# Moving all but three DMA issues of a transpose kernel from SyncE to ScalarE's own queue

## The chip, the cores and the metric

One core of one Trainium2 chip. The time is device microseconds of one execution; the median of several is given. The kernels were checked for the right result on the chip.

## The reference

```python
def setup_inputs():
    return {"x": np.random.randn(8192, 8192).astype(np.float32)}

def reference(x):
    return np.transpose(x)
```

256 MiB in, 256 MiB out, no arithmetic.

## The kernel before

The input is cut into two column halves of 4096 columns, and each half into 64 chunks of 128 rows: 128 chunks, each loaded by one DMA of 2 MiB into one of three input buffers. TensorE transposes a chunk in eight groups of four 128x128 tiles, each group into one of eight PSUM tiles. ScalarE copies the even groups out of PSUM and VectorE the odd ones, into output regions that gather eight chunks, so that the rows written to memory are 4 KB long. In each ordinary chunk one region is complete and is stored by one DMA of 2 MiB; there are nine regions for eight open ones. SyncE issues all loads and stores, in the order store of chunk t, load of chunk t+3.

The loop, cut to what the change touches (`# ...` marks cuts):

```python
def load(t):
    s, c = chunks[t]
    nc.sync.dma_start(
        out=ins[t % NIN], in_=x[c * P:(c + 1) * P, s * J:(s + 1) * J]
    ).then_inc(s_ld[t % NIN], 16)

for t in range(NIN):          # NIN = 3
    load(t)
# ...
for t, (s, c) in enumerate(chunks):
    nc.tensor.wait_ge(s_ld[t % NIN], 16 * (t // NIN + 1))
    closing = []
    for q in [(c + k) % NR for k in range(NR)]:
        if q not in window:
            # ... take a region r; if it was used before:
            (nc.scalar, nc.vector)[q % 2].wait_ge(s_st[r], 16 * stored[r])
        # ... wait for the PSUM tile, four transposes, last.then_inc(s_pe, 1); n += 1
        (nc.scalar, nc.vector)[e].wait_ge(s_pe, n)       # e = q % 2
        # ... copy to the region, then_inc(s_cp[e], 1)
        if t + 1 == t0 + sum(z - a for _, a, z in parts):
            closing.append((q, e, copied[e]))
    for q, e, count in closing:
        nc.sync.wait_ge(s_cp[e], count)
        # ... one DMA per part of the region, on nc.sync
    if t + NIN < len(chunks):
        nc.sync.wait_ge(s_pe, n)
        load(t + NIN)
```

At the seam between the two column halves a region belongs to both, and is stored by two DMAs with shorter rows.

## Time and profile before

| | before |
|---|---|
| time | 1265.68 us median of 3 (1265.38 to 1265.71) |
| profiled span | 1263.6 us |
| bytes moved by the kernel | 536.9 MB, plateau about 429 GB/s |
| busy: TensorE, VectorE, ScalarE | 59%, 28%, 24% |
| load, issue to landing (median) | 23.6 us |
| full-size store, issue to landing (median) | 22.6 us |

How to read it: "issue to landing" is the time from the instruction that starts a DMA to its last completion signal, "slice" a fortieth of the span, "plateau" the slices at a steady rate, and "the pipe" the DMA engines taken together. The compute engines are far from busy (59% at most), the DMA engines are busy in every slice (90% or more in 39 of 40, 80% or more in the last). The prediction below shows the lines.

### The profile page before, as it was taken

Reading aid. Unit: us, or ns where it says so; the run is one execution under the profiler, and the core shown is the slowest. Engines: PE = TensorE matmul, PEld = TensorE weight load, DVE = VectorE, ACT = ScalarE, POOL = GpSimd, SP = SyncE. Lnnn points to the kernel's source line nnn. Section 1 sums busy time; section 2 is a strip of 40 time slices with the busy share of each in tenths; the row PEclk is TensorE's granted clock in tenths of the full one; section 3 lists DMA queues with packets and bytes.
Section 4 is the critical chain, followed back from the end, with each engine's and each line's share of the span. In section 5 each row is a group of like instructions: output and inputs, shape, how many; then the busy total and the mean of one; then the engine's idle time right before and its main releaser. Section 6 shows DMA issues by size and latency. Waiting matters only on the chain.

```text
span 1263.6 us, 9807 instructions
## 1 busy us (share of the span) xinstructions
PE 748.9 (59%) x4096; PEld 724.9 (57%) x4096; DVE 353.9 (28%) x512; ACT 301.2 (24%) x513; POOL 0.7 (0%) x6
## 2 busy tenths in 40 slices
PE   6666555665566656565566655665556656565561
PEld 5566555665566656565566655665555655565551
DVE  3322222232222322222222322222222322223220
ACT  3222222222222222222222222222222222222220
POOL 0000000000000000000000000000000000000000
PEclk9876868677677776868677767777777686868776
DMA  9999999999999999999999999999999999999998
GB/s 385 427 427 430 428 427 430 429 430 429 428 428 428 430 429 429 428 430 429 427 427 412 430 429 428 429 429 429 429 429 429 429 429 427 431 429 429 430 427 351
DMA packets 39308, 537.51 MB, mean 425 GB/s; under 512 B 4320, under 2 KB 4832, under 8 KB 6240
## 3 DMA queue, kind: packets, MB, share of 16 engines
q1 hardware_dynamic: 39264, 536.89, 99.9%
q8 instruction: 32, 0.52, 0.2%
q14 instruction: 12, 0.10, 0.0%
HBM read 268.44 MB, written 268.44 MB: 425 GB/s over the span
## 4 chain that ended last, share of the span: by engine, by line
DMA 78%; PE 19%; issue 0%; ACT 0%; SPq 0%; ACTq 0%
DMA in<-in_x_dram 78%; PE ps L139 19%; ACT reg L150 0%; SPq L209 0%; SPq L69 0%; ACTq L148 0%
## 5 line engine op out<-in xcount | busy, mean ns | idle before, releaser
L139 PE MATMUL ps<-ident,in 128*128 128x128 f32 x4096 | 748.9, 365 | 486.8 <-DMA in<-in_x_dram 486.8
L139 PEld LDWEIGHTS ps<-ident,in 128*128 128x128 f32 x4096 | 724.9, 219 | 510.7 <-DMA in<-in_x_dram 502.4
L152 DVE COPY reg<-ps 128x512 f32<-128x512 f32 x512 | 353.9, 691 | 882.1 <-PE ps L139 882.1
L150 ACT COPY reg<-ps 128x512 f32<-128x512 f32 x512 | 299.9, 586 | 934.3 <-PE ps L139 932.6
L150 ACT ACT_TABLE_LOAD x1 | 1.3, 1283 | 0.9 <-SPq L69 0.9
L84 POOL TENSOR_SCALAR_AFFINE_SELECT ident<-ident 128x128 f32<-128x128 f32 x1 | 0.3, 292 | 0.2 <-POOL ident L82 0.2
L82 POOL MEMSET ident<- 128x128 f32 x1 | 0.2, 204 | 0.5 <-SPq L69 0.5
L198 POOL MEMSET const-bfloat16-1.0<- 128x1 bf16 x1 | 0.1, 101 | 0.0
L198 POOL MEMSET const-uint8-127<- 128x1 uint8 x1 | 0.1, 101 | 0.0
L198 POOL MEMSET const-float32-0.0<- 128x1 f32 x1 | 0.1, 98 | 0.2 <-issue 0.2
L198 POOL MEMSET const-float32-1.0<- 128x1 f32 x1 | 0.1, 98 | 0.0
## 6 DMA issues: line engine op xcount, KB each, us to landing
in<-in_x_dram SPq DMA_DIRECT2D x128, 2048.0 KB, 23.6
out_dram<-reg SPq DMA_DIRECT2D x114, 2048.0 KB, 22.6
out_dram<-reg SPq DMA_DIRECT2D x4, 1792.0 KB, 19.9
out_dram<-reg SPq DMA_DIRECT2D x4, 1536.0 KB, 19.6
out_dram<-reg SPq DMA_DIRECT2D x4, 1280.0 KB, 19.6
out_dram<-reg SPq DMA_DIRECT2D x4, 1024.0 KB, 19.4
out_dram<-reg SPq DMA_DIRECT2D x4, 768.0 KB, 17.9
out_dram<-reg SPq DMA_DIRECT2D x4, 512.0 KB, 16.2
```

Source lines behind the costliest of these rows:

```text
L82: nc.gpsimd.memset(ident, 0.0).then_inc(s_id, 1)
L84: nc.gpsimd.affine_select(out=ident, in_=ident, compare_op=mybir.AluOpType.not_equal, fill=1.0, base=0, pattern=[[-1, P]], channel_multipl ...
L139: last = nc.tensor.transpose(ps[:, b * P:(b + 1) * P], ins[t % NIN][:, q * B * P + b:(q + 1) * B * P - B + b + 1:B], ident,)
L150: cp = nc.scalar.copy(out=o, in_=i)
L152: cp = nc.vector.tensor_copy(out=o, in_=i)
L198: nc = _bacc.Bacc("TRN2", target_bir_lowering=False, num_devices=1)
```

## The change

The intent, in the words that came with it: loads and stores are all issued by ScalarE on its own queue, and SyncE issues only the first three loads and holds almost no program. ScalarE issues a finished region's store after its next copy, so that it never waits for the copy it has just started.

```diff
-            nc.sync.dma_start(
+            (nc.sync if t < NIN else nc.scalar).dma_start(
                 out=ins[t % NIN], in_=x[...]
...
+        def store(q, e, count):
+            t0, r, parts = window.pop(q)
+            nc.scalar.wait_ge(s_cp[e], count)
+            # ... the same DMAs as before, on nc.scalar ("qActDynamicHW")
+            free.append(r)
...
                 cp.then_inc(s_cp[e], 1)
+                if e == 0:
+                    for k in closing:
+                        store(*k)
+                    closing = []
                 if t + 1 == t0 + sum(z - a for _, a, z in parts):
                     closing.append((q, e, copied[e]))
-            for q, e, count in closing:
-                nc.sync.wait_ge(s_cp[e], count)
-                # ... the DMAs on nc.sync
+            for k in closing:
+                store(*k)
             if t + NIN < len(chunks):
-                nc.sync.wait_ge(s_pe, n)
+                nc.scalar.wait_ge(s_pe, n)
                 load(t + NIN)
```

More of the change, by code (lines that the diff above doesn't have):

```diff
@@ L111 @@
         window = {}
-        stores = 0
+        def store(q, e, count):
+            t0, r, parts = window.pop(q)
+            nc.scalar.wait_ge(s_cp[e], count)
+            base = 0
+            for s, a, z in parts:
+                rows = (z - a) * P
+                j0 = s * J + q * B * P
+                dst = out[j0:j0 + B * P, a * P:a * P + rows]
+                dst = dst.rearrange("(q b) i -> q b i", q=P)
+                src = regs[r][:, base:base + B * rows]
+                base += B * rows
+                if any(stored):
+                    st = wide_dma(nc, nc.scalar, "qActDynamicHW", dst, src)
+                else:
+                    st = nc.scalar.dma_start(
+                        out=dst, in_=src.rearrange("q (b i) -> q b i", b=B)
+                    )
+                st.then_inc(s_st[r], 16)
+                stored[r] += 1
+            free.append(r)
         for t, (s, c) in enumerate(chunks):
@@ L155 @@
                 bank[(n - 1) % NPS] = (s_cp[e], copied[e])
+                if e == 0:
+                    for k in closing:
+                        store(*k)
+                    closing = []
                 if t + 1 == t0 + sum(z - a for _, a, z in parts):
                     closing.append((q, e, copied[e]))
-            for q, e, count in closing:
-                t0, r, parts = window.pop(q)
-                nc.sync.wait_ge(s_cp[e], count)
-                base = 0
-                for s_, a, z in parts:
-                    rows = (z - a) * P
-                    j0 = s_ * J + q * B * P
-                    dst = out[j0:j0 + B * P, a * P:a * P + rows]
-                    dst = dst.rearrange("(q b) i -> q b i", q=P)
-                    src = regs[r][:, base:base + B * rows]
-                    base += B * rows
-                    if stores:
-                        st = wide_dma(nc, nc.sync, "qSPDynamicHW", dst, src)
-                    else:
-                        st = nc.sync.dma_start(
-                            out=dst, in_=src.rearrange("q (b i) -> q b i", b=B)
-                        )
-                    st.then_inc(s_st[r], 16)
-                    stores += 1
-                    stored[r] += 1
-                free.append(r)
+            for k in closing:
+                store(*k)
             if t + NIN < len(chunks):
-                nc.sync.wait_ge(s_pe, n)
+                nc.scalar.wait_ge(s_pe, n)
                 load(t + NIN)
```

## The prediction

> **What bounds the kernel now.** I read the page first (busy shares, slices, DMA queues, chain), then the waits of the compute engines and of SyncE's queue, then the chain in order of time, then the timeline around one ordinary chunk of rows, one chunk at the seam between the two column halves, and the tail.
>
> The page of the kernel before:
>
> ```profile
> span 1263.6 us, 9807 instructions
> PE 748.9 (59%) x4096; PEld 724.9 (57%) x4096; DVE 353.9 (28%) x512; ACT 301.2 (24%) x513; POOL 0.7 (0%) x6
> ...
> DMA  9999999999999999999999999999999999999998
> GB/s 385 427 427 430 428 427 430 429 430 429 428 428 428 430 429 429 428 430 429 427 427 412 430 429 428 429 429 429 429 429 429 429 429 427 431 429 429 430 427 351
> ...
> q1 hardware_dynamic: 39264, 536.89, 99.9%
> q8 instruction: 32, 0.52, 0.2%
> q14 instruction: 12, 0.10, 0.0%
> ```
>
> No compute engine is over 60% busy; the DMA row is full in every slice. The 536.89 MB of queue 1 at the plateau of 429 GB/s need 1251.5 us. The span is 12.1 us longer: the first slice (31.6 us at 385 instead of 429) loses 3.2 us, the last (351) 5.7 us, slice 22 (412) 1.3 us, and the slices at 427 and 428 the rest. The kernel is a full transfer pipe with a start, an end and one small dip.
>
> The chain of waits names loads (78%) and TensorE (19%), which could be misread as a latency problem: a load can be issued only when TensorE has finished the chunk that lay in its buffer, three chunks earlier. In order of time:
>
> ```profile
> 347.55 6.50 PE ps L139 x32
> 354.07 22.71 DMA in<-in_x_dram
> 376.83 5.60 PE ps L139 x32
> 382.45 23.61 DMA in<-in_x_dram
> 406.11 6.28 PE ps L139 x32
> 412.40 22.94 DMA in<-in_x_dram
> ```
>
> The columns are start, length, what. TensorE's part varies with the granted clock, from 5.60 to 6.50 us, and the load's part gives it back: 6.50 + 22.71 = 29.21, 5.60 + 23.61 = 29.21, 6.28 + 22.94 = 29.22. A load issued 0.9 us later lands at the same moment. The turn is 3 x 9.74 us, three chunks at the pipe's pace: one chunk moves 2.10 MB in and 2.10 MB out, 4.19 MB / 429 GB/s = 9.78 us. So 23 us from issue to landing is not latency but queue: 23.6 us x 429 GB/s = 10.1 MB, 2.4 chunks of work in front of every new transfer. This is a natural experiment on exactly what the change does, and I lean on it most.
>
> The waits, compute engines first, then SyncE's queue (us in total, times, longest):
>
> ```profile
> ACT reg L150 <- PE ps L139: 932.6, 510, 7.3
> PE ps L139 <- DMA in<-in_x_dram: 486.8, 127, 8.3
> ACT reg L150 <- DMA out_dram<-reg: 1.7, 2, 1.1
> ...
> SPq L99 <- PE ps L139: 467.1, 125, 8.8
> SPq L28 <- DVE reg L152: 318.8, 65, 9.2
> ```
>
> ScalarE idles 932.6 us for TensorE, so it has room; it waited only twice, 1.7 us in all, for a store to free an output region.
>
> [...]
>
> **The change, part by part.**
>
> 1. Issue time moves. SyncE loses 125 loads and 142 stores. An ordinary store issue takes 0.545 us (the median of the tile view of the output), a load issue 0.34 us: 142 x 0.545 + 125 x 0.34 = 120 us. ScalarE's 301 us become about 421 us, 33% of the span. Off the path: 0.
>
> 2. Stores leave later. Each chunk closes one region, with its first group. Before, SyncE issues as soon as that copy is done; now ScalarE issues after its next copy. An ordinary chunk before:
>
> ```profile
> 611.07 6.20 PE L139 MATMUL ps<-ident,in 128*128 128x128 f32 x32 [4.16 <-DMA in<-in_x_dram]
> 612.23 0.59 ACT L150 COPY reg<-ps 128x512 f32<-128x512 f32 x1 [4.65 <-PE ps L139]
> 612.85 1.22 SPq L28 DMA_DIRECT2D out_dram<-reg  x2
> 613.09 0.69 DVE L152 COPY reg<-ps 128x512 f32<-128x512 f32 x1 [5.93 <-PE ps L139]
> 613.94 0.59 ACT L150 COPY reg<-ps 128x512 f32<-128x512 f32 x1 [1.12 <-PE ps L139]
> ...
> 617.30 0.34 SPq L99 DMA_DIRECT2D in<-in_x_dram  x1
> ```
>
> Where ScalarE made the first copy, its next ends at 613.94 + 0.59 = 614.53, so the store goes 1.7 us later; where VectorE did, about 0.6 us later. The order of stores and loads in the queue is the same (store of chunk t, then load t+3), and 20 us of work lie ahead of them. Cost: 0.
>
> 3. Loads leave 0 to 0.6 us later: in every other chunk ScalarE has the last copy to start first. Absorbed as in the chain above. Issue-to-landing falls by 0.3 us for loads and 1.2 us for stores; the landings stay. Cost: 0.
>
> 4. The seam. From 622 to 686 us each region is stored by two DMAs with short rows, and the issuing instruction blocks:
>
> ```profile
> 627.26 6.37 SPq L99 DMA_DIRECT2D in<-in_x_dram  x1
> 633.90 2.92 SPq L28 DMA_DIRECT2D out_dram<-reg  x2
> 638.10 5.94 SPq L99 DMA_DIRECT2D in<-in_x_dram  x1
> ```
>
> [...] Now ScalarE stands still there. Copies 4 x 0.59 = 2.4 us, stores about 2.5, load about 5.5: 10.4 us in a 9.8 us chunk, for some seven chunks. ScalarE falls behind by one or two us, but blocking means the pipe is full[...]. TensorE has eight PSUM tiles, a whole chunk's groups, so ScalarE must be a chunk late before TensorE stops. Cost 0 to 1.5 us; I take 0.3.
>
> 5. The tail. The last ten store issues take 41.04 us on SyncE, blocked in the same way. On ScalarE the last chunk's four copies (4 x 0.59) stand between them. The pipe is full whenever the issue blocks, and the copies are made before the stores that need them. Cost 0 to 2 us; I take 0.3.
>
> 6. The start. [...] The bytes are the same and the pipe stays full. Cost -0.5 to +1; I take 0.
>
> 7. SyncE's program. Its 267 DMA instructions and their waits go to ScalarE; the fetched bytes hardly change, and all of queue 14 is 0.10 MB, 0.0% of the DMA time. Gain at most a few tenths; I take -0.4.
>
> Sum: 0.3 + 0.3 - 0.4 = +0.2 us on 1265.68, so 1265.9 us.
>
> **Rivals.**
>
> Rival A, ScalarE becomes the bound: it is blocked in issues, the copies starve and TensorE waits for PSUM. For: the 6.37 us blocks. Against: only some seven chunks and the tail block, and 932.6 us of idle time are spare. If ordinary issues also blocked (a load issue of 3 us or more on this queue), 128 chunks could lose 1 us each: 1390 us.
>
> Rival B, region reuse becomes a wait that holds back loads. A store issued 1.7 us into chunk t lands 22.6 us later (median), at 24.3; its region is reopened by the last group of chunk t+2, finished at 19.5 + 5.6 = 25.1 or later. The margin is under 1 us, and the stores now leave 0.6 to 1.7 us later. If landing followed issue, ScalarE would wait up to 0.9 us in half of the chunks, with a load behind it. Against: landing follows queue position, not issue; and a load 1 us late costs nothing. At worst, the queue of 23 us gets 1 to 2 us shorter: 1266 to 1268 us.
>
> Rival C, it gets faster, because fetches for SyncE or its waits held the queue up. It needs a hole in the pipe to fill, and the plateau has none: only slice 22, the start and the end are below it. Removing the whole dip gives 1.3 us: 1264.4 us.
>
> **Range and chances.** Repeated runs lie within 0.33 us. The uncertain terms (seam, tail, start, fetch) reach from about -2 to +3 us together: 1263.2 to 1268.9. A gain of 2% (25 us) would be twice all the time above the plateau, so 0.01. A loss of 2% needs rival A in ordinary chunks: 0.03. Within 2%: 0.96.
>
> **What would show it.** Right: plateau again 427 to 430 GB/s; TensorE plus load in the chain again 29.2 us a turn; ScalarE's waits for stores still a handful; load issue-to-landing 23.0 to 23.6 us and stores about 21.5; the blocked load issues near 640 us now on ScalarE's queue. Wrong: plateau under 425; TensorE waiting for ScalarE's copies; ScalarE waiting dozens of times for stores; ordinary load issues well over 0.34 us; a longer end than the 5.7 us lost in the last slice.

Measured, for what the text says without a number: the three TensorE parts of 6.50, 5.60 and 6.28 us had granted clocks of 0.57, 0.70 and 0.60. "The pipe is full" where an issue blocks: from 622 to 686 us, with load issues of 4.4 to 6.4 us, 422 GB/s at a busy share of the DMA engines of 1.01; from 1230 to 1254.8 us, where the last store issues took up to 4.7 us, 416 GB/s at 0.99.

## The result

| | before | changed |
|---|---|---|
| time, median of 6 | 1265.72 us (1265.38 to 1266.00) | 1265.89 us (1265.30 to 1266.48) |
| profiled span | 1263.6 us | 1263.6 us |
| load, issue to landing (median) | 23.6 us | 23.5 us |
| all stores, issue to landing (median) | 22.6 us | 21.9 us |
| full-size stores alone | 22.6 us | 22.4 us |
| instruction packets of queue 14 | 12 | 12 |

The ratio is 1.0001 with a 95% interval of 0.9988 to 1.0014. A ratio here is the mean time of one kernel's runs over the mean of the other's in the same rounds, so not quite the ratio of the medians. The page of the changed kernel:

```profile
GB/s 385 426 428 430 429 427 430 429 428 430 428 430 428 429 428 431 428 430 430 427 425 412 431 428 429 429 429 430 428 429 429 430 429 427 429 428 431 428 428 353
...
q10 hardware_dynamic: 38832, 530.60, 98.7%
q1 hardware_dynamic: 432, 6.29, 1.2%
...
q14 instruction: 12, 0.10, 0.0%
```

The data has moved to another queue (10, ScalarE's; queue 1 keeps SyncE's three loads of 2.10 MB), and the row of GB/s (that of before is in the prediction) is the same to within 2: the same first slice, dip and last slice. The same chunk as in the prediction, in order of time. It is the first of the second half, so its region is already stored by two DMAs (the x2); up to the first store's issue, and in its load's short issue, it is like an ordinary one:

```profile
610.96 5.60 PE L160 MATMUL ps<-ident,in 128*128 128x128 f32 x32 [4.17 <-DMA in<-in_x_dram]
611.75 0.58 ACT L171 COPY reg<-ps 128x512 f32<-128x512 f32 x1 [4.28 <-PE ps L160]
...
613.18 0.58 ACT L171 COPY reg<-ps 128x512 f32<-128x512 f32 x1 [0.85 <-PE ps L160]
613.19 1.21 ACTq L28 DMA_DIRECT2D out_dram<-reg  x2
...
616.60 0.33 ACTq L99 DMA_DIRECT2D in<-in_x_dram  x1
```

The store's issue begins 0.01 us after the second copy of 0.58 us has begun, not after its end; so it was over the ordinary chunks (median 0.01 us after the start of a copy, 101 stores). So the store leaves later than before by less than I had worked out. Over some 100 ordinary chunks, from TensorE's first transpose to the store's issue: 1.76 us before, 2.37 us changed, 0.61 us later on average (1.1 us where ScalarE made the first copy, 0.15 us where VectorE did). Loads leave 0.09 us later (median, counted from TensorE's last transpose).

The seam and the last chunk:

```profile
627.33 6.86 ACTq L99 DMA_DIRECT2D in<-in_x_dram  x1
632.02 5.71 PE L160 MATMUL ps<-ident,in 128*128 128x128 f32 x32 [5.13 <-DMA in<-in_x_dram]
...
634.22 1.25 ACT L171 COPY reg<-ps 128x512 f32<-128x512 f32 x2 [6.32 <-PE ps L160]
...
1240.96 0.58 ACT L171 COPY reg<-ps 128x512 f32<-128x512 f32 x1 [4.68 <-issue]
```

ScalarE stands in a load's issue for 6.86 us, until 634.19, while TensorE starts the next chunk at 632.02; it then makes two copies back to back, and TensorE does not notice. The very last copy starts at 1240.96 us. Before:

```profile
1235.81 0.58 ACT L150 COPY reg<-ps 128x512 f32<-128x512 f32 x1 [0.44 <-PE ps L139]
```

Five microseconds later, and the span is the same.

The waits of the changed kernel (us in total, times, longest):

```profile
ACT reg L171 <- PE ps L160: 928.3, 502, 7.2
...
PE ps L160 <- DMA in<-in_x_dram: 485.6, 127, 8.3
...
ACT reg L171 <- issue: 4.8, 2, 4.7
...
ACT reg L171 <- DMA out_dram<-reg: 1.9, 2, 1.1
```

TensorE waits for loads only, for 485.6 us as against 486.8 before. ScalarE's waits for stores are still two.

### The profile page after: what moved, and what is told of

The parts are those of the page before. It is cut to its first block, busy times and chain, and to the rows that moved or that the text cites. A ratio compares the mean times of both kernels' runs of the same rounds, so it can differ in the third digit from the quotient of the medians.

```text
span 1263.6 us, 9807 instructions
## 1 busy us (share of the span) xinstructions
PE 750.0 (59%) x4096; PEld 725.9 (57%) x4096; DVE 353.8 (28%) x512; ACT 300.9 (24%) x513; POOL 0.7 (0%) x6
## 4 chain that ended last, share of the span: by engine, by line
DMA 78%; PE 18%; ACT 1%; ACTq 0%; issue 0%; DVE 0%; SPq 0%
DMA in<-in_x_dram 76%; PE ps L160 18%; DMA out_dram<-reg 2%; ACT reg L171 1%; ACTq L28 0%; DVE reg L173 0%; ACTq L169 0%; SPq L216 0%; SPq L69 0%
## 5 line engine op out<-in xcount | busy, mean ns | idle before, releaser
L160 PE MATMUL ps<-ident,in 128*128 128x128 f32 x4096 | 750.0, 366 | 485.6 <-DMA in<-in_x_dram 485.6
## 6 DMA issues: line engine op xcount, KB each, us to landing
in<-in_x_dram ACTq DMA_DIRECT2D x125, 2048.0 KB, 23.5
out_dram<-reg ACTq DMA_DIRECT2D x114, 2048.0 KB, 22.4
```

The lines of the kernel that those rows point to most:

```text
L160: last = nc.tensor.transpose(ps[:, b * P:(b + 1) * P], ins[t % NIN][:, q * B * P + b:(q + 1) * B * P - B + b + 1:B], ident,)
```

## The experiments

The theory was that of the prediction: two chunks of work are queued in front of every transfer, so who issues and when does not matter (2.4 chunks, by the prediction's estimate from 23.6 us and 429 GB/s). Its rivals: that a gain and a loss cancel; that the changed kernel is near a cliff; that issue delay is on the path, as the chain suggests. Eleven kernels were run: first the two one-part kernels, a filler and a hold; then a shorter filler and two later holds; then two pairs.

### Loads alone, stores alone

```diff
 # e1: from the kernel before
-            nc.sync.dma_start(            # in load(t)
+            (nc.sync if t < NIN else nc.scalar).dma_start(
-                nc.sync.wait_ge(s_pe, n)
+                nc.scalar.wait_ge(s_pe, n)
 # e2: from the changed kernel
-            (nc.sync if t < NIN else nc.scalar).dma_start(
+            nc.sync.dma_start(
-                nc.scalar.wait_ge(s_pe, n)
+                nc.sync.wait_ge(s_pe, n)
```

> Only the loads after the first three move to ScalarE; the stores stay on SyncE[...]. Theory (the pipe is full and has two chunks of work queued, so the issuer does not matter): 1265.7 us, within 1 us of before, plateau 427 to 430 GB/s. Since loads no longer stand behind stores in one queue, their time to landing may leave 23.5 us, but TensorE's part plus the load's part stays 29.2 us a turn. Rival (a gain from the emptier SyncE program cancels a loss from ScalarE's blocked issues): loads alone bring the loss of the seam without the full gain, so at least 1 us slower than before.

> Only the stores move to ScalarE; all loads stay on SyncE. Theory: 1265.7 us within 1 us, plateau 427 to 430 GB/s, TensorE's part plus the load's part 29.2 us a turn. Rival (gain and loss cancel): ScalarE blocks only in stores and SyncE's program halves, so a gain of 1 us or more, or, with the sign of run e1, a change opposite to it. [...]

Measured: loads alone 1264.92 us (1263.85 to 1269.03, ratio to before 0.9998, 0.9985 to 1.0012); stores alone 1265.27 us (1264.21 to 1267.87, ratio 0.9997, 0.9984 to 1.0009). Neither leaves the time of before, and they don't have opposite signs, so nothing shows a gain in one part that a loss in the other takes back; an effect under about 1.5 us would not be seen.

Something smaller is left open. Eight of these ten runs (1263.85 to 1265.55 us) lie below all nine runs of before beside them (1265.63 and more), and two lie well above (1267.87 and 1269.03). And the dip at the seam, which is 427 and 412 GB/s in slices 21 and 22 before, is nearly filled: 423 and 426 in e1, 427 and 424 in e2, worth 0.7 to 0.9 us at 429 GB/s. The row of e2:

```profile
GB/s 386 428 430 429 429 429 430 427 430 429 428 430 429 428 430 429 430 426 430 428 427 424 427 429 429 428 430 430 427 430 429 430 428 429 429 429 430 429 427 356
```

So the dip was smaller in both runs that have loads in one queue and stores in the other; with the two high runs, a gain is not shown. (q1 is SyncE's queue in the pages, q10 ScalarE's.)

My detail that a turn stays TensorE plus load did not hold. With loads and stores in two queues, the wait moved to other places. The waits of the kernel with stores alone:

```profile
DVE reg L173 <- DMA out_dram<-reg: 373.4, 31, 13.5
...
ACT reg L171 <- DMA out_dram<-reg: 190.9, 30, 6.8
...
PE ps L160 <- ACT reg L171: 116.0, 32, 7.7
```

Before, these were 0, 1.7 and 0 us. The copies now wait 564 us for stores to free their regions, and TensorE waits for the copies. This is the wait of the prediction's rival B, though not its reason: e1 has it too (374 us), where SyncE still issues the stores, while the changed kernel, which issues them late, has 2.3 us of it. What e1 and e2 share is the two queues. And the wait costs nothing: the pipe still moves 429 GB/s, and TensorE's waits sum to 486 us in e2 (253.9 for loads, 232.0 for copies) and 493 us in e1, after 486.8 us before, all for loads. The same slack is booked to other waits.

### A long program in SyncE

```diff
 # e3: the changed kernel; s_fill is a semaphore that nobody reads
+                nc.sync.wait_ge(s_pe, n)
+                for _ in range(16):        # f1: range(4)
+                    nc.sync.nop().then_inc(s_fill, 1)
                 nc.scalar.wait_ge(s_pe, n)
                 load(t + NIN)
```

> The changed kernel, with 16 semaphore increments a chunk put into SyncE's program, some 2,000 instructions that do nothing. Theory: queue 14 goes from 12 packets of 8 KB to about 27, 0.22 MB, and the time stays at 1265.9 us within 0.7 us. Rival (SyncE's program and its fetches cost something that the change removed): fifteen fetches where before had two, so several times whatever the change gained; 2 us or more slower.

(The two fetches of before are a guess from packet times; see step 7 below.)

Measured: 1276.64 us (1274.40 to 1277.88), ratio to before 1.0083 (1.0069 to 1.0097). My theory missed: SyncE's program is not free. The page:

```profile
GB/s 383 426 425 429 421 429 429 429 428 428 430 429 427 430 428 430 429 428 430 427 422 415 428 429 431 429 428 430 429 428 427 430 427 425 422 428 420 415 375 302
...
q14 instruction: 28, 0.23, 0.0%
```

The plateau holds for 33 slices and then crumbles: 420, 415, 375, 302. That is no steady cost but something that shows at the end. The trace has 16 landing times for a DMA, one for each piece of it, but not which DMA engine moved a piece, nor whether the piece that is last time after time is the same one. Sorting the 16 landings of single DMAs by time, and writing each relative to the last (my computation from the landing records; the first column is about the time in the span, us):

```
before      1227  -7.35 -7.34 -7.29 -7.08 -6.92 -4.97 -4.04 -3.70 -0.94 -0.84 -0.83 -0.75 -0.61 -0.30 -0.02 0
changed     1228  -7.42 -7.31 -7.27 -7.02 -6.96 -5.37 -3.89 -3.81 -1.14 -0.91 -0.73 -0.37 -0.36 -0.21 -0.04 0
16 a chunk  1002 -14.70 -14.69 -14.48 -14.07 -14.02 -11.60 -10.97 -9.82 -9.79 -9.43 -9.21 -8.97 -8.04 -7.75 -7.60 0
16 a chunk  1240 -12.99 -12.86 -12.75 -12.61 -12.36 -11.86 -11.46 -11.34 -11.10 -11.08 -11.06 -10.99 -10.97 -9.19 -9.16 0
 4 a chunk  1228  -7.20 -7.18 -6.89 -6.37 -6.01 -3.95 -3.93 -3.70 -1.56 -1.55 -1.26 -1.15 -0.60 -0.23 -0.05 0
```

In before and changed alike, the last piece lands 7.4 us behind the first, with the others spread in between. With the filler a single piece is far behind all the others, by 9.2 us at 1240 us and still by 6.0 us in the very last store. These 6.0 us are half of the 12.5 us by which the profiled span is longer (1276.1 after 1263.6). The other fifteen pieces of that store are late too (1268.8 us; before, all had landed by 1262.3); why is argued, not shown: the kernel waits for all 16 pieces (TensorE starts 0.05 us after the last one, at 376.83 us after 376.78 in before), so a late piece also delays what is issued next.

The last piece's distance to the first grows by about 1.2 us for each 8 KB of SyncE's program (79 us of the span), of which some 0.35 us are there in before and changed too. Its distance to the middle of the 16 pieces does not grow there; here it grows by 0.73 us, nearly all in one step at each packet of the instruction queue that comes with the filler (a fetch, for short). For instance it goes from 3.94 to 4.62 us between the DMAs that land at 427.7 and 433.3 us, with a fetch at 428 us. So a second theory: SyncE's program makes the last of the 16 pieces lag by about 0.9 us for each 8 KB (14.7 us behind the first, over 16 packets), and costs only what goes beyond the 7.4 us that are there anyway. It needs its own test, with a shorter program (in the recorded text its wording is cut, since it put the lag down to a DMA engine, which the trace does not name):

> The changed kernel with 4 instead of 16 empty semaphore increments a chunk on SyncE, some 500 instructions, about 4 fetches of 8 KB. The 16-increment run was 10.8 us slower, against the theory[...]. Theory 2[...]: a quarter of the lag, under 4 us, stays hidden, 1265.9 us within 0.7 us. Rival (each fetch lengthens the path by 0.7 us): 4 fetches, 1268.6 us.

Measured: 1265.74 us (1265.59 to 1266.23), ratio 1.0000 (0.9986 to 1.0013). With 16 instruction packets instead of 12 and some 500 more instructions there is no cost, and the last row of the table shows no lonely piece. The rival of 1268.6 us is excluded. That the fetch makes the step is read from its time alone; no run has the same instructions without the fetches.

### Holding ScalarE back

```diff
 # e4: the changed kernel; junk is a buffer of its own
+                for k in range(4):   # f2: 4 if t >= 12 else 0;  f3: 8 if t >= 12 else 0
+                    nc.scalar.wait_ge(s_jk, jk)
+                    nc.scalar.copy(out=junk, in_=junk).then_inc(s_jk, 1)
+                    jk += 1
+                nc.scalar.wait_ge(s_jk, jk)
                 nc.scalar.wait_ge(s_pe, n)
                 load(t + NIN)
```

> The changed kernel, with four idle copies of 128x1024 on ScalarE before each load's issue, each waiting for the one before; by twice the columns of the 0.586 us copies I estimate 1.0 to 1.2 us each, so each load leaves 4 to 5 us later. Theory (a late issue is given back by the queue): 1266 us within 2 us, load issue to landing from 23.5 down to about 19 us, plateau still 427 to 430 GB/s, ScalarE about 850 us busy. Rival (each microsecond of issue delay is on the path, as the chain of waits through TensorE and loads seems to say): a turn of three chunks gets 4.5 us longer, 43 turns, so about 1450 us.

Measured: 1270.75 us (1269.43 to 1272.03), ratio 1.0038 (1.0025 to 1.0052). Far from the rival's 1450, but outside my 2 us. In the plateau it went as expected (429 GB/s, loads landing 18.8 us after issue), but the first slice moved only 338 GB/s instead of 385 and the second 418: there the queue is still short (in the changed kernel the first eight loads take 7 to 18 us from issue to landing, against 23.5 in the median). The row of the page:

```profile
GB/s 338 418 426 429 426 428 428 428 426 428 427 429 429 428 425 430 427 429 428 428 421 418 430 429 429 430 429 429 429 429 429 429 430 428 429 429 430 429 429 343
```

47 of 429 GB/s for 31.6 us are 3.5 us, and with the second slice some 4.2 of the 4.9 us. The next run leaves the start alone:

> The run with four idle copies before each load was 4.9 us slower, not 0. I read that as lost at the start, where the queue is still short (338 GB/s in the first slice instead of 385, 3.5 us, and 418 in the second), not in the plateau. Here the copies begin with chunk 12. Theory: 1266.5 us within 1.5 us, first slice 385 again, load issue to landing 18.8 us as in that run. Rival (the hold, or ScalarE's longer program, costs 5 us along the way): 1270 us.

Measured: 1266.15 us (1265.60 to 1266.33), ratio 1.0001 (0.9987 to 1.0015). Its issue table:

```profile
in<-in_x_dram ACTq DMA_DIRECT2D x125, 2048.0 KB, 18.8
```

From 23.5 to 18.8: the loads leave 4.5 us later than in the changed kernel (mean of the ordinary chunks), and that is taken out of their time in the queue, and the landings stay. So the miss was the start, as read.

> Eight idle copies of 1.05 us from chunk 12 on. ScalarE needs 8 x 1.05 + 4 x 0.59 = 10.8 us a chunk, with gaps about 11.0, over the pipe's 9.76. Theory: now ScalarE is the bound, 113 chunks x 1.3 us more, 1395 to 1430 us, plateau about 380 GB/s, issue to landing of loads far below 18 us. If issue delay as such were free without limit: 1266 us.

Measured: 1414.71 us (1413.43 to 1416.49), ratio 1.1176, as predicted from 10.8 us of ScalarE's work a chunk. Its waits, where neither line was there before:

```profile
PE ps L165 <- ACT reg L176: 349.8, 96, 6.8
...
PEld ps L165 <- ACT reg L176: 50.4, 54, 2.4
```

This is the cliff. The changed kernel uses 2.4 us for copies and about 0.9 us for issues of a chunk's 9.76 us, so it stands well away from it.

### No queue to hide in

```diff
 # e6: the kernel before;  e7: the changed kernel
-    NIN = 3
+    NIN = 1
```

> The kernel before with one input buffer instead of three: a load is issued only when TensorE has emptied the only buffer, so no queue stands in front of it but the store of the same chunk. Estimate: TensorE 4.2 to 5.6 us, then the rest of the store and the load of 4.9 us, some 12 to 14 us a chunk, 1550 to 1800 us, plateau near 330 GB/s. It is the base for the next run.

> The changed kernel with one input buffer. Theory (the change makes stores and loads leave 0.2 to 0.6 us later, and only the queue hides that): here the delay shows, 128 chunks x 0.2 to 0.5 us, so 25 to 65 us slower than the one-buffer kernel that issues from SyncE. Rival (ScalarE issues as promptly as SyncE, so nothing had to be hidden): the same time within 10 us.

Measured: 1847.61 us (1846.78 to 1848.91) with SyncE, 1931.37 us (1929.21 to 1932.68) with ScalarE, on the same chip. I had the base 50 us too low and the difference too small: it is 84 us, 0.65 us a chunk, against 0.2 to 0.5 expected. The traces have the size: with one buffer the store leaves 2.45 us after TensorE's start instead of 1.83 us, 0.62 us later, and the load, which stands behind it in the same queue, lands later by about as much. This is the 0.61 us by which the change delays stores in the original kernel. And the two kinds of chunk tell it apart (means over 93 ordinary chunks, computed from the traces): where ScalarE makes the first copy, the store leaves 1.10 us later and the chunk takes 15.46 us instead of 14.21; where VectorE makes it, 0.14 us later, and 14.42 us instead of 14.27. So the change does make issues later; with three buffers the queue swallows it, and with one it costs 4.5%.

### ScalarE blocked in every chunk

```diff
 # e8: the kernel before;  e9: the changed kernel, on nc.scalar
+    if rows == W * P:                      # ordinary region: two DMAs of half the row length
+        src = src.rearrange("q (b i) -> q b i", b=B)
+        wide_dma(..., dst[:, :, :rows // 2], src[:, :, :rows // 2]).then_inc(s_st[r], 16)
+        stored[r] += 1
+        dst, src = dst[:, :, rows // 2:], src[:, :, rows // 2:]
     st = wide_dma(..., dst, src)
```

> The kernel before, each ordinary store cut into two DMAs with rows of 2 KB instead of 4 KB: twice the rows of every chunk, as in the seam. From the ordinary chunks (2.3 stores of 512 rows and 2.4 loads of 128 rows in flight, 1485 rows, no block) and the seam (about 2660, blocked) I estimate that the queue takes some 2000 rows. So SyncE's issues should block in every chunk (load issues of 4 us and more, median), and the time be that of the pipe: 1266 to 1290 us, by how much slower rows of 2 KB are. It is the base for the next run.

> The same cut stores in the changed kernel, so ScalarE blocks in every chunk, not in seven. Theory (a blocked issuer means a full pipe): within 3 us of the cut kernel that issues from SyncE; TensorE waits for ScalarE's copies at most a few us in all. Rival A of the prediction (blocked ScalarE starves the copies): TensorE waits for ScalarE in most chunks and the time is at least 25 us longer than with SyncE as issuer.

Measured: 1296.00 us (1294.82 to 1297.68) with SyncE, 1294.64 us (1294.08 to 1295.34) with ScalarE. The cut stores with their shorter rows cost more than I allowed (30 us; the plateau is 418 GB/s, with 143,232 packets instead of 39,264), but that is the same for both. The tile view of the loads (duration of an issue in ns, minimum, median, maximum) and the waits, with ScalarE issuing:

```profile
L99 ACTq DMA_DIRECT2D in<-in_x_dram x125: 334/5164/9702, 14.0 to 1238.2; - x125
```

```profile
ACT reg L176 <- issue: 550.9, 135, 8.7
```

The median load issue takes 5.2 us, ScalarE spends 551 us of its idle time before copies in issues, and in the list of waits TensorE does not wait for ScalarE at all. Rival A, blocked issues that starve the copies, had its best chance here and cost nothing (1294.64 us with ScalarE as issuer, 1296.00 with SyncE). Here blocked issues go with a pipe at its plateau of 418 GB/s. The 2000 rows of the expectation stay an estimate from its two row counts (1485 without long issues, about 2660 with them).

## Why the prediction was right

1265.9 us were predicted, 1265.89 measured. A hit to 0.01 us is luck beside a spread of 1.2 us between runs; the steps count.

- **The full pipe with a queue of two chunks.** Shown. Later by 4.5 us is free (f2), and without the queue 0.6 us a chunk is not (e7 against e6).
- **Step 1, 120 us of issues off the path.** Holds: TensorE never waited for ScalarE.
- **Step 2, stores 1.7 or 0.6 us later.** Mis-sized: 1.1 and 0.15 us, since the issue follows the start of ScalarE's next copy and not its end. The consequence, 1.2 us less from issue to landing (about 21.5 us), came out at 21.9 us for all stores, and at 22.4 for the full-size ones alone, from which the 22.6 was read. No effect on the time, as said.
- **Step 3, loads 0 to 0.6 us later.** 0.09 us in the median, for the same reason.
- **Steps 4 and 5, seam and tail, 0.3 us each.** Not seen: slice 22 is 412 in both, the last slice 353 after 351. That ScalarE's blocked issues cost nothing is shown by e9 over the whole run (1294.64 us after 1296.00 with SyncE). One reading was wrong: the 41.04 us of the last ten store issues are a row of the timeline from the first one's start to the last one's end, idle time included. The ten issues themselves sum to 21.8 us, and only the last six of them (19.7 us) took longer than usual.
- **Step 6, the start.** TensorE took the third load up at 18.18 us after 18.13 before, so it did not land later to speak of. The first slice is 385 in both.
- **Step 7, SyncE's program, -0.4 us.** No gain seen. Fetched packets are 12 and 12, as I had argued (the trace does not name the engine that a packet is for; from their times I guess that two of those before, at 338 and 932 us, are SyncE's, and that ScalarE's go from five to seven). But I had argued from the wrong quantity: 0.0% of the DMA time did not tell what such packets cost. With a program of 2,000 instructions and 16 packets more it was 10.8 us (e3). That the two packets I take for SyncE's were harmless before is argued from f1, where four cost nothing.
- **Rival B**: its wait came in the kernels with two queues (374 and 564 us), with early stores (e1) as with late ones (e2), and was free there too. **Rival C** had no hole in the plateau to fill: no run that moved issues or SyncE's program was faster than before beyond noise. The one hole that any run seems to have filled is the dip at the seam, in e1 and e2.
- **Smaller slips that changed nothing.** The chunk at 611 us, called ordinary, is the first with two stores. The slices outside the first, the last and slice 22 lose 0.8 us against 429 GB/s, and not the rest of the 12.1 (1.9): the row of GB/s also counts 0.62 MB of instructions. And -2 to +3 us around 1265.68 is a little less than the range given.

## What to carry to other kernels

Before moving DMA issues, look at the time from issue to landing and at the GB/s row. Here 23.6 us were 2.4 chunks of transfers and the row was flat at 429 GB/s, and a load issued 4.5 us later was given back (f2); even an issuer blocked for 5.2 us in the median load issue was harmless (e9), and one whose own work of 10.8 us exceeded the chunk's 9.76 us was not (f3, 1414.71 us). The chain of waits named loads for 78% of the span, and yet delaying their issue cost nothing: it names the wait that ends last, not the bound; check it by adding a delay. And a program's packets, 0.0% of the DMA time, must be judged by a run and not by that share: 16 more of them came with 10.8 us (e3), four more with none (f1).
